# Retention issued ahead of the RWKV projections in a two-layer hybrid backbone

## The chip, the cores and the metric

The kernel runs on one core of one Trainium2 chip. The metric is the device time of one execution in microseconds (us). It is given as the median of several runs; single executions that were profiled carry a trace from which the rows below are taken. TensorE is called PE in the rows, VectorE DVE, ScalarE ACT, GpSimd POOL, and SP is the engine that issues nearly all transfers.

## What is computed

A backbone of two layers (DEPTH 2) over 1024 latent tokens and 256 context tokens of width 1024. Every layer projects the modulated tokens once, feeds four mixers of 256 columns each (mLSTM, Hyena, retention, RWKV-7), joins them by an output projection, and ends with a convolutional feed-forward part. Retention and RWKV-7 are independent of each other; each scans forward and backward. The parts of the reference that matter here:

```python
def token_mixer(u, uc, p, ang, need_ctx):
    parts = split_columns(u @ p['w_in'])
    parts_c = split_columns(uc @ p['w_in'])
    ...
    yr, yr_c = retention_mixer(parts[8:12], parts_c[8:12], ang, gs(2, ng), gs(2, nb))
    yw, yw_c = rwkv_mixer(parts[12:18], parts_c[12:18], p['rwkv_mu'], ...)
    y = jnp.concatenate([ya, yb, yr, yw], -1).astype(u.dtype) @ p['w_out']

# retention, per chunk of 128 tokens
s = jnp.einsum('bhid,bhjd->bhij', qc, kc) * decay_mask
o = jnp.einsum('bhij,bhjd->bhid', s, vc) + jnp.einsum('bhid,bhde->bhie', qc * q_dec[..., None], s_mem)
s_new = s_mem * chunk_dec[:, None, None] + jnp.einsum('bhjd,bhje->bhde', kc * k_dec[..., None], vc)

# the front of RWKV-7
z = token_shift(jnp.concatenate(seq_parts, -1).astype(F32), mu)
r, k, v, wlo, alo, glo = jnp.split(z, list(RWKV_SPLIT), axis=-1)
g = jax.nn.sigmoid(glo) @ g2
kk = kk * lax.rsqrt(jnp.sum(kk * kk, -1, keepdims=True) + 1e-12)
bonus = jnp.sum(rh * kh * rk[None, :, None, :], -1, keepdims=True) * vh
```

The second layer (called layer 1) puts out the latent tokens alone, 8 tiles of 128; layer 0 all 10 tiles.

## The kernel before

`layer` (line 1353) runs the mixers' front one after the other: Hyena, the projections of mLSTM and of retention (which write to memory), then `rwkv_front`, then `retention`, then the scans of RWKV-7 and mLSTM together, the output projection and the feed-forward part. All instructions go through a scheduler that keeps each engine's queue in an order of its own, worked out from a simulated timeline; an engine then executes its queue strictly in that order. The order of the code sets the priority and the order in which buffers are handed out.

`rwkv_front` (line 376) makes seven projections of 128 columns, in the order j = 6, 2, 3, 4, 5, 0, 1. Each is `proj` (line 1050): a weight block is loaded, split into a high and a low part (lines 1015 and 1016), and multiplied in three passes (lines 1022, 1023, 1024) for token blocks of 512, 512 and 256, which makes 72 matmuls; ScalarE moves each block out (line 1061). `seg_conv` (line 347, operations at 352, 354, 355 on VectorE) shifts along the tokens. What follows a projection is deferred behind the next one: for j=6 the gates (matmuls at line 397), for j=2 and 3 the keys and their norms by a matmul with a block of ones (line 406), for j=4 and 5 the values and their transposes (line 1104), for j=0 and 1 the bonus: r is stored to memory (`wrk`, line 415), the key and value are loaded (417, 419), multiplied (418), summed by the ones (matmul 422) and stored (423 to 424 on VectorE).

`retention` (line 796) loads queries, keys and values by 30 transfers (28 in layer 1; line 803). It rotates queries and keys of eight tiles: two products on GpSimd (line 812), two operations on VectorE (813, 814) for each. It forms k2 (818) and multiplies it with the values (matmul 820, copied out at 822) for all ten tiles. GpSimd then scans the states, 16 times a product and a sum (826, 827). Then each tile's output follows: transposes (832, 838), scores (846) masked on VectorE (849), and two products of the scores and the state (852, 853), and after every two tiles a group norm and a store of `yr` (line 659).

After that `close_u` gives back the projected input, `psum` deals out the PSUM banks anew, and `rwkv` begins: it loads what the front stored (`rkk`, line 480, from `wrk`; TWA, VSA), multiplies on VectorE (lines 500 to 530, the product with the loaded keys at 515), transposes a matrix (550), and inverts it step by step (557, 558). The wide scans with which `mlstm` begins (lines 693 to 704) stand on the same VectorE queue.

```python
            rwkv_front(k,l,pv,pvr,last)
            with k.tc.tile_pool(name="rt",bufs=1,side="right") as k.p_rt:
                retention(k,l,last)
        close_u(k)
        psum(k,cbank=2,ybank=1,pbank=1,dbank=2,mbank=2)
```

Of the kernel before, what the change touches and what calls it, by code (L numbers as in the profile page):

```python
# [310 lines left out]
def hyena_proj(K,l,pv,last):  # L311
    NT=8 if last else 10
    for j in range(6):
        z=proj(K,l,1040+j*128,not last,K.bank if l and j<0 else None)
        zc=K.p_tmp.tile([128,1280],F32,tag="tmpA",name="zc",bufs=2)
        w=(pv['hw'][:,j:j+1],pv['hw'][:,6+j:7+j],pv['hw'][:,12+j:13+j],pv['hb'][:,j:j+1])
        seg_conv(K,lambda o,n: zc[:,o:o+n],z,w,ctx=not last)
        later(K,lambda zc=zc,j=j: z_tokens(K,zc,NT,dram=K.D['hyx'][:,j*128:j*128+128],pad=False))
    later(K)
# [38 lines left out]
def rwkv_params(k,l,pv,p):  # L358
    nc=k.nc; tt=nc.vector.tensor_tensor
    c0=p.tile([128,7],F32,name="c0")  # L360
    tt(out=c0,in0=pv['mu0'],in1=pv['mu1'],op=ALU.add)
    nc.vector.tensor_scalar(out=c0,in0=c0,scalar1=-1.0,scalar2=1.0,op0=ALU.mult,op1=ALU.add)
    G2=p.tile([128,256],F32,name="G2"); nc.sync.dma_start(G2[64:128],k.a['rwkv_g2'][l])
    return c0,G2
# [530 lines left out]
def params_mix(k,l,pool):  # L895
    a=k.a
    v1=lambda n: a[n][l:l+1].rearrange("o (j p) -> (o j) p",p=128)
    mu=a['rwkv_mu'][l]
    specs=[('mw',rows(a['mlstm_conv_w'][l]),12),('mb',v1('mlstm_conv_b'),4),('hw',rows(a['hyena_conv_w'][l]),18),('hb',v1('hyena_conv_b'),6),
           ('mu0',rows(mu[0:1]),7),('mu1',rows(mu[1:2]),7),('kk',v1('rwkv_kk'),2),('ka',v1('rwkv_ka'),2),  # L900
           ('rk',a['rwkv_rk'][l:l+1].rearrange("o h d -> (o h d)").rearrange("(j p) -> j p",p=128),2),
           ('ng',v1('out_norm_g'),8),('nb',v1('out_norm_b'),8)]
    return load_rows(k,specs,"pvm%d"%l,pool)
# [394 lines left out]
def open_u(k):  # L1298
    k.ucm=k.tc.tile_pool(name="u",bufs=1,side="right"); pu=k.ucm.__enter__()
    k.uh=pu.tile([128,8,1280],F32R,name="uh"); k.ul=pu.tile([128,8,1280],F32R,name="ul")  # L1300


def close_u(k):
    k.ucm.__exit__(None,None,None)
# [14 lines left out]
def mlstm_proj(k,l,pv,last,js=range(8)):  # L1319
    nc=k.nc; D=k.D; nfull=1024 if last else 1280  # L1320
    for j in js:
        z=proj(k,l,j*128,(not last) or 2<=j<6)
        if j<4:
            t=k.p_tmp.tile([128,1280],F32,tag="tmpA",name="mt",bufs=2)
            seg_conv(k,lambda o,n: t[:,o:o+n],z,(pv['mw'][:,j:j+1],pv['mw'][:,4+j:5+j],pv['mw'][:,8+j:9+j],pv['mb'][:,j:j+1]),ctx=(not last) or j>=2)
            n=1024 if (last and j<2) else 1280
            nc.scalar.activation(out=t[:,:n],in_=t[:,:n],func=ACTF.Silu)
            if j<2: nc.vector.tensor_scalar(out=t[:,:n],in0=t[:,:n],scalar1=0.125,scalar2=None,op0=ALU.mult)
            store_fm(k,D['mqk'][j*128:j*128+128],t,False,n)
        elif j<6: later(k,lambda z=z,j=j: z_tokens(k,z,10,dram=D['mv'][:,(j-4)*128:(j-4)*128+128]))  # L1330
        else:
            later(k)
            n=1025 if last else 1282
            nc.scalar.activation(out=z[:,1:n],in_=z[:,1:n],func=ACTF.Sigmoid)
            store_fm(k,D['go'][(j-6)*128:(j-6)*128+128],z,True,nfull)
    later(k)


def filters(k,l):
    with k.tc.tile_pool(name="hf",bufs=1,side="right") as k.p_hf, k.tc.tile_pool(name="hfy",bufs=1,side="right") as k.p_hy:  # L1340
        for L in ((1024,256) if l==0 else (1024,)): hyena_filter(k,l,L,k.Ds[l]['ks' if L==1024 else 'ksc'])
# [11 lines left out]
def layer(k,l,out):  # L1353
    nc=k.nc; last=l==1
    D=k.D=k.Ds[l]; k.Dn=k.Ds[l+1] if not last else None
    with ExitStack() as es:
        P=lambda **kw: es.enter_context(k.tc.tile_pool(**kw))
        pl=P(name="pl",bufs=1)
        pv=params_mix(k,l,pl)
        with ExitStack() as ed:  # L1360
            P2=lambda **kw: ed.enter_context(k.tc.tile_pool(**kw))
            if l: pg=P2(name="pg",bufs=1)
            k.p_w=P2(name="w",bufs=1); k.p_z=P2(name="z",bufs=1); k.p_tmp=P2(name="tmp",bufs=1)
            if not l: pg=P2(name="pg",bufs=1)
            pvr=rwkv_params(k,l,pv,pg)
            k.bones=pg.tile([128,128],F32,name="bones"); nc.sync.dma_start(k.bones,k.a['c_bones'])
            k.sum16=pg.tile([32,16],F32,name="sum16"); nc.sync.dma_start(k.sum16,k.a['c_sum16'])
            GT=gates(k,l,pg,pl)
            hyena_proj(k,l,pv,last)
            if l>0: filters(k,l)  # L1370
            with k.tc.tile_pool(name="hy",bufs=1,side="right") as k.p_hy:
                hyena(k,l,pv,last)
            mlstm_proj(k,l,pv,last,range(0,8))
            ret_proj(k,l,pv,last,range(0,8))
            rwkv_front(k,l,pv,pvr,last)
            with k.tc.tile_pool(name="rt",bufs=1,side="right") as k.p_rt:
                retention(k,l,last)
        close_u(k)
        psum(k,cbank=2,ybank=1,pbank=1,dbank=2,mbank=2)
        with ExitStack() as ew:  # L1380
            with ExitStack() as er:
                R=lambda **kw: er.enter_context(k.tc.tile_pool(bufs=1,side="right",**kw))
                p1=R(name="r1"); p2=R(name="r2"); pa=R(name="pa"); e3=ExitStack(); p3=e3.enter_context(k.tc.tile_pool(name="r3",bufs=1,side="right"))
                with k.tc.tile_pool(name="ml",bufs=1) as k.p_ml:
                    k.J=k.p_ml.tile([128,128],F32,name="J"); nc.sync.dma_start(k.J,k.a['c_J'])
                    scan=rwkv(k,l,pv,last,p1,p2,p3)
                    for _ in range(2): next(scan)
                    side=ada_steps(k,[(l,g) for g in range(2,6)]+[(1,g) for g in range(2) if l==0],pa,k.mbank,17 if last else 19)
                    mlstm(k,l,GT,last,side)
                pw=ew.enter_context(k.tc.tile_pool(name="pw",bufs=1))  # L1390
                wo=[[pw.tile([128,1024],F32R,name="wo%d%d"%(q,i)) for i in range(2)] for q in range(8)]
                for _ in scan: pass
                e3.close()
                load_wo(k,l,wo,p2.tile([128,8,256],F32,tag="G",name="wst",bufs=3))
                ep=ExitStack(); pb=ep.enter_context(k.tc.tile_pool(name="pb",bufs=1))
            psum(k,bank=5,dbank=3)
            open_u(k)
            mix_out(k,l,pv,last,wo,pl,pb,ep)
    ffn(k,l,last,out)
# [46 lines left out]
```

## Time and profile before

| | |
|---|---|
| time, median of 3 runs | 4264.0 us (4252.06 to 4266.33) |
| the profiled execution: own time | 4269.9 us |
| its span, first to last instruction | 4268.0 us |
| granted TensorE clock, mean | 0.940 |
| PE busy | 3956.8 us (93%) |
| DVE busy | 2672.2 us (63%) |
| ACT busy | 1416.9 us (33%) |
| POOL busy | 979.7 us (23%) |

The shares are means over the whole span, over stages of very different kinds. The granted clock is the share of TensorE's full speed that the chip allowed; its levels are 1.2 and 2.4 GHz. A row of the timeline that stands for several instructions gives the time from the first's start to the last's end, and the starts of two rows tell how long the first really held the engine, since matmuls overlap. A single-precision matmul of the code stands as two in the trace, so the 40 key-value products of line 820 are 80 there.

### The profile page before, as it was taken

What the parts mean: (1) busy time and instruction counts of PE and PEld (TensorE: products, weight loads), DVE (VectorE), ACT (ScalarE), POOL (GpSimd) and SP (SyncE); (2) the same over time, 40 slices, a digit from 0 to 9 for tenths busy, and PEclk for the clock granted to TensorE, in tenths of its full rate; (3) what the DMA queues carried; (4) which work ended last, traced back from release to release, by engine and by line L of the source; (5) the groups of instructions that cost most, each with busy time, mean ns of one, the idle gap of its engine ahead of it and who ended that gap; (6) DMA issues with size and microseconds to landing.
All of it is one profiled execution on the core that took longest, in us unless ns stands there. A gap on an engine that the chain in (4) does not pass through costs nothing.

```text
span 4268.0 us, 65334 instructions
## 1 busy us (share of the span) xinstructions
PE 3956.8 (93%) x24976; PEld 3210.9 (75%) x24976; DVE 2672.2 (63%) x5412; ACT 1416.9 (33%) x2855; POOL 979.7 (23%) x2158
## 2 busy tenths in 40 slices
PE   5999999699979999999997999996899899999998
PEld 3878877566668888888884688885666678888886
DVE  5655665789769444444449555676888684444447
ACT  4433343554344211211123433344544342112121
POOL 3320023466512000000021221024666320000002
PEclk6999999789989999999998999997899699999999
DMA  4235444343343111111113235553332431111112
GB/s 166 74 102 177 149 153 122 112 143 116 122 160 119 45 40 34 41 40 35 37 35 124 82 91 154 169 162 114 122 115 84 136 114 55 48 41 55 45 50 99
DMA packets 477138, 414.16 MB, mean 97 GB/s; under 512 B 48827, under 2 KB 443284, under 8 KB 474010
## 3 DMA queue, kind: packets, MB, share of 16 engines
q1 hardware_dynamic: 476826, 409.99, 31.0%
q8 instruction: 197, 3.23, 0.3%
q14 instruction: 115, 0.94, 0.1%
HBM read 323.65 MB, written 86.25 MB: 96 GB/s over the span
## 4 chain that ended last, share of the span: by engine, by line
PE 52%; DVE 11%; DMA 3%; issue 2%; POOL 1%; ACT 1%; SPq 0%; ACTq 0%; DVEq 0%; POOLq 0%
PE bank L1022 9%; PE bank L1023 9%; PE bank L1024 9%; PE dbank L1022 6%; PE dbank L1023 6%; PE dbank L1024 6%; DVE bst L983 1%; DMA xt<-x 1%; DVE facc L1205 1%; PE bank L186 1%; PE bank L187 1%; DMA wst<-in_w_out 1%; PE dbank L529 0%; DVE facc L1206 0%; DVE facc L1274 0%
## 5 line engine op out<-in xcount | busy, mean ns | idle before, releaser
L1022 PE MATMUL dbank<-uh,wh 128*128 128x512 f32 (+1 forms) x2120 | 765.3, 370 | 8.8 <-ACT tmpB L398 5.7
L1023 PE MATMUL dbank<-ul,wh 128*128 128x512 f32 (+1 forms) x2120 | 761.2, 368 | 0.0
L1016 DVE TENSOR_TENSOR wl<-wst,wh 128x1024 fp32r<-128x1024 f32 x146 | 185.5, 1272 | 491.9 <-ACT wh L1015 367.3
L1024 PE MATMUL dbank<-uh,wl 128*128 128x512 f32 (+1 forms) x2120 | 480.6, 367 | 0.0
L1022 PEld LDWEIGHTS dbank<-uh,wh 128*128 128x128 f32 x2120 | 401.4, 189 | 85.0 <-ACT tmpB L398 6.1
L1023 PEld LDWEIGHTS dbank<-ul,wh 128*128 128x128 f32 x2120 | 401.6, 189 | 68.9 <-issue 1.1
L1024 PEld LDWEIGHTS dbank<-uh,wl 128*128 128x128 f32 x2120 | 365.9, 188 | 70.5 <-issue 1.5
L1264 DVE TENSOR_TENSOR facc<-facc,bank 128x512 f32<-128x512 f32 x324 | 221.8, 686 | 205.1 <-PE bank L1024 205.1
L1022 PE MATMUL bank<-uh,wh 128*128 128x512 f32 (+1 forms) x920 | 334.9, 372 | 4.5 <-ACT uh L1010 4.5
L1233 POOL MEMSET fz<- 128x1 f32 x132 | 7.2, 98 | 1433.6 <-DVE fc L1248 1433.6
L1023 PE MATMUL bank<-ul,wh 128*128 128x512 f32 (+1 forms) x920 | 335.1, 372 | 0.8 <-DVE ul L1011 0.8
L1022 PE MATMUL bank<-wdh,gh 128*128 128x512 f32 x792 | 314.9, 400 | 17.9 <-DVE facc L1278 8.7
L1023 PE MATMUL bank<-wdl,gh 128*128 128x512 f32 x792 | 310.5, 392 | 1.0 <-DVE wdl L1016 1.0
L1024 PE MATMUL bank<-wdh,gl 128*128 128x512 f32 x792 | 248.1, 392 | 0.0
L1015 ACT ACTIVATE wh<-wst 128x1024 fp32r<-128x1024 f32 x146 | 154.8, 1060 | 238.1 <-PE dbank L1023 168.4
L1015 ACT ACTIVATE wdh<-wst 128x1024 fp32r<-128x1024 f32 x46 | 48.8, 1062 | 529.4 <-PE bank L1024 427.7
L558 POOL TENSOR_TENSOR XL<-XL,lt 128x48 f32<-128x48 f32 (+26 forms) x620 | 204.4, 330 | 47.7
L557 POOL TENSOR_TENSOR lt<-LM,XL 128x48 f32<-128x48 f32 (+26 forms) x620 | 187.1, 302 | 119.4 <-ACT XL L551 45.0
L1024 PE MATMUL bank<-uh,wl 128*128 128x512 f32 (+1 forms) x920 | 211.9, 372 | 0.0
L1022 PEld LDWEIGHTS bank<-uh,wh 128*128 128x128 f32 x920 | 174.1, 190 | 36.1 <-ACT uh L1010 5.6
L1023 PEld LDWEIGHTS bank<-ul,wh 128*128 128x128 f32 x920 | 174.2, 189 | 31.9 <-DVE ul L1011 1.7
L1022 PEld LDWEIGHTS bank<-wdh,gh 128*128 128x128 f32 x792 | 149.7, 189 | 59.4 <-DVE facc L1278 14.9
(476 smaller groups left out, 8132.3 us busy)
## 6 DMA issues: line engine op xcount, KB each, us to landing
wst<-in_ffn_w_up SPq DMA_DIRECT2D x88, 512.0 KB
adaw<-in_ada_w SPq DMA_DIRECT2D x160, 256.0 KB
wst<-in_w_in SPq DMA_DIRECT2D x58, 512.0 KB
wst<-in_ffn_w_down SPq DMA_DIRECT2D x46, 512.0 KB
df<-in_c_F SPq DMA_DIRECT2D x10, 1344.0 KB
xt<-x SPq DMA_DIRECT2D x26, 512.0 KB
df<-in_c_I SPq DMA_DIRECT2D x8, 1344.0 KB
rkk<-wrk SPq DMA_DIRECT2D x10, 1024.0 KB
```

The costliest lines, as they stand in the source:

```text
L186: mm(dst_re,F[:,i],pre(slot),start=True,stop=False); mm(dst_re,F[:,i+1],pim(slot),start=False,stop=True)
L187: mm(dst_im,F[:,i],qim(slot),start=True,stop=False); mm(dst_im,F[:,i+2],qre(slot),start=False,stop=True)
L557: e.tensor_tensor(out=t_,in0=LM[:,j,j+1:32].unsqueeze(2).to_broadcast([128,n,m]),in1=X[h][:,j:j+1,0:m].to_broadcast([128,n,m]),op=A.mult)
L558: e.tensor_tensor(out=X[h][:,j+1:32,0:m],in0=X[h][:,j+1:32,0:m],in1=t_,op=A.add)
L983: for h in range(2): nc.vector.bn_stats(out=st[:,h],in_=x[h])
L1015: k.nc.scalar.activation(out=h,in_=st,func=ACTF.Copy)
L1016: k.nc.vector.tensor_tensor(out=lo,in0=st,in1=h,op=ALU.subtract)
L1022: mm(ps,lh,rh,start=(i==0),stop=False)
L1023: mm(ps,lh,rl,start=False,stop=False)
L1024: for i,((lh,ll),(rh,rl)) in enumerate(pairs): mm(ps,ll,rh,start=False,stop=(i==n-1 and more is None))
L1205: for o,i,gg in zip([y[:,h] for h in hs],x,[g[:,h] for h in hs]) if parts else [(y,x,g)]: stt(out=o,in0=i,scalar=m,in1=gg,op0=ALU.subtract ...
L1264: else: tt(out=d,in0=d,in1=ps,op=ALU.add)
```

## The change

`rwkv_front` is called after `retention` instead of before it, inside the scope of retention's buffers. It is the same in both layers. The buffers of retention therefore live until the front is through. Nothing else is edited.

```diff
             ret_proj(k,l,pv,last,range(0,8))
-            rwkv_front(k,l,pv,pvr,last)
             with k.tc.tile_pool(name="rt",bufs=1,side="right") as k.p_rt:
                 retention(k,l,last)
+                rwkv_front(k,l,pv,pvr,last)
         close_u(k)
         psum(k,cbank=2,ybank=1,pbank=1,dbank=2,mbank=2)
```

What the scheduler makes of it on PE, in layer 0 behind the projection j=2: line 397 is the gates, line 820 the key-value products (`k_...` is the k2 of one tile), lines 1022 and 1023 the projection j=3. The piece is the difference, and goes on with 71 more matmuls of j=3 taken out here.

```order
 L397 MATMUL dbank<-tmpA,G_1691 128x512 x2
 L397 MATMUL dbank<-tmpA,G_1691 128x256
+L820 MATMUL bank<-rqkv_5194,k_5228 128x64 x4
+L820 MATMUL bank<-rqkv_5194,k_5237 128x64 x4
+L820 MATMUL bank<-rqkv_5194,k_5256 128x64 x4
+L820 MATMUL bank<-rqkv_5194,k_5274 128x64 x4
 L397 MATMUL dbank<-tmpA,G_1691 128x512 x2
 L397 MATMUL dbank<-tmpA,G_1691 128x256
-L1022 MATMUL dbank<-uh,wh 128x512
-L1023 MATMUL dbank<-ul,wh 128x512
```

Behind them in the new order stand the other six groups of line 820, with one pair of the projection's matmuls in between, then the first transposes of retention's tiles (832, 838), and from there on one tile of retention for about every 24 matmuls of the projections j=3, 4 and 5. The projections j=0 and 1 and the bonus of both come last. In layer 1 seven of the ten groups stand behind the projection j=4 and before the norm matmuls of j=3.

SP's queue in layer 0, at the end of the front: `wrk` is the memory that holds r, k and kk (line 415 stores r of j=0 and then j=1, line 480 loads them as `rkk`). Before:

```order
L415 DMA wrk_100<-tmpA 1280x1x128
L1125 DMA bv_93<-tmpB 128x1280
L417 DMA tmpB<-wrk_100 64x10x128 x2
L419 DMA tmpB<-wvf_102 128x1280
L1125 DMA bv_93<-tmpB 128x1280
L659 DMA yr_88<-rqkv_6024 128x2x256 x4
L479 DMA TWA<-twa_103 64x128 x2
L659 DMA yr_88<-rqkv_6024 128x2x256
L1385 DMA J<-in_c_J 128x128
L480 DMA rkk<-wrk_100 128x2048
```

Now:

```order
L415 DMA wrk_100<-tmpA 1280x1x128
L1125 DMA bv_93<-tmpB 128x1280
L484 DMA VSA<-wv_101 64x2x256
L484 DMA SV<-wv_101 64x2x256
L479 DMA TWA<-twa_103 64x128 x2
L480 DMA rkk<-wrk_100 128x2048
```

The stores of `yr` have moved ahead, among the stores of the front, and the load of `rkk` stands a few transfers behind the store of r (j=1), where five stores of `yr` and the bonus of j=1 stood between before.

VectorE's queue in layer 0, around the transposition of line 550, before (lines 697 to 704 belong to mLSTM):

```order
L697 TENSOR_TENSOR mVO<-mIG,mB 8x1280
L696 TENSOR_TENSOR mVO<-mB,mM 8x1280
L530 TENSOR_TENSOR G<-dbank,rmask 128x512
L702 TENSOR_TENSOR me<-mB,mM 8x10
L503 TENSOR_TENSOR lw<-cs 128x520
L515 TENSOR_TENSOR bk<-bk,rkk 128x4x64 x2
L700 TENSOR_TENSOR mW<-mVO,mM 8x1280
L515 TENSOR_TENSOR bk<-bk,rkk 128x4x64 x2
L703 TENSOR_TENSOR me<-me,mM 8x10
L704 TENSOR_TENSOR mIG<-mVO,me 8x1280
L550 STREAM_TRANSPOSE LM<-NB 128x1024
```

and now (lines 423 and 424 are the bonus of j=1):

```order
L423 TENSOR_TENSOR tmpB<-dbank,tmpB 128x512 x2
L423 TENSOR_TENSOR tmpB<-dbank,tmpB 128x256
L500 SCALAR_TENSOR_TENSOR lw<-ex,lw 128x8x64
L424 TENSOR_SCALAR tmpB<-tmpB,pvm_1661 128x1280
L502 SCALAR_TENSOR_TENSOR cs<-smask,lw 128x260 x2
L530 TENSOR_TENSOR G<-dbank,rmask 128x512 x2
L503 TENSOR_TENSOR lw<-cs 128x520
L535 STREAM_TRANSPOSE NB<-G 32x128 x4
L671 CAST identb<-ident 128x128
L530 TENSOR_TENSOR G<-dbank,rmask 128x512 x2
L550 STREAM_TRANSPOSE LM<-NB 128x1024
L557 TENSOR_TENSOR lt<-LM,XL 128x15
```

The mLSTM operations (lines 693 to 704) have moved behind line 550, and the bonus of j=1 stands before it.

## Rows read from the trace of the kernel before

**Rows 1.** The page, part 4, of the whole span: the chain's shares by engine.

```profile
PE 52%; DVE 11%; DMA 3%; issue 2%; POOL 1%; ACT 1%; SPq 0%; ACTq 0%; DVEq 0%; POOLq 0%
```

**Rows 2.** Windows: start:end, length, busy us (count) by engine, PE clock, DMA, GB/s.

```profile
580.47:608.70 28.23, 28.23 (x146) 23.69 (x144) 13.17 (x15) 15.69 (x18) 1.29 (x9) 1.00 0.64 197
608.70:640.00 31.30, 25.62 (x115) 19.43 (x115) 30.45 (x47) 11.76 (x22) 22.63 (x37) 0.89 0.50 151
640.00:707.00 67.00, 67.00 (x371) 56.73 (x370) 37.12 (x44) 24.27 (x41) 22.16 (x30) 1.00 0.51 134
707.00:764.00 57.00, 50.56 (x338) 42.64 (x336) 32.79 (x62) 19.69 (x41) 22.01 (x29) 0.85 0.25 81
764.00:806.00 42.00, 18.78 (x146) 15.37 (x147) 32.75 (x51) 26.76 (x58) 15.95 (x28) 0.72 0.62 167
800.00:1000.00 200.00, 172.65 (x2084) 131.05 (x2085) 175.13 (x551) 102.46 (x313) 129.91 (x373) 0.86 0.42 129
2838.00:2858.00 20.00, 19.67 (x110) 16.38 (x110) 17.90 (x27) 11.02 (x18) 12.30 (x21) 1.00 0.95 286
2888.50:2944.00 55.50, 46.74 (x311) 38.64 (x309) 35.67 (x59) 19.75 (x42) 29.28 (x37) 0.85 0.26 79
```

**Rows 3.** Timeline of PE: start, length, instruction, xcount, [idle before, its releaser].

```profile
608.70 4.56 PE L397 MATMUL dbank<-tmpA,G 64*128 64x512 f32 x12
618.94 0.79 PE L1022 MATMUL dbank<-uh,wh 128*128 128x512 f32 x1 [5.67 <-ACT tmpB L398]
...
654.51 1.89 PE L820 MATMUL bank<-rqkv,k 128*128 128x64 f32 x16
...
723.14 0.69 PE L853 MATMUL bank<-rSS,rT 128*128 128x64 f32 x2 [2.10 <-POOL rSS L827]
...
738.56 0.60 PE L832 MATMUL bank<-ident,rqkv 128*128 128x128 f32 x4
...
742.79 0.61 PE L832 MATMUL bank<-ident,rqkv 128*128 128x128 f32 x4
...
2837.82 2.31 PE L406 MATMUL dbank<-tmpB,bones 128*128 128x512 f32 x6
```

**Rows 4.** Timeline of DVE from 608 to 636: first rotation, a convolution, last rotation.

```profile
609.27 0.66 DVE L813 TENSOR_TENSOR rqkv<-rqkv,crcos 128x256 f32<-128x256 f32 x1 [1.89 <-DMA rqkv<-rqkv]
609.86 1.47 DVE L354 SCALAR_TENSOR_TENSOR tmpA<-z,pvm,tmpA 128x1024 f32<-128x1024 f32 x1
...
635.18 0.43 DVE L814 TENSOR_TENSOR rqkv<-rqkv,rtmp 128x256 f32<-128x256 f32 x1
```

**Rows 5.** Groups by line, DVE, from 608.7 to 636: the k2 products.

```profile
L818 DVE TENSOR_TENSOR k<-rqkv,crKD 128x512 f32<-128x512 f32 x4 | 3.4, 874 | 0.0
```

**Rows 6.** Groups by line, POOL: 608.7 to 764, then (layer 1) 2841 to 2918.

```profile
L812 POOL TENSOR_TENSOR rtmp<-rqkv,crsin 128x128 f32<-128x128 f32 x32 | 21.1, 688 | 14.5 <-DMA rqkv<-rqkv 11.1 <-issue 2.5 <-POOL rtmp L812 0.8
L827 POOL TENSOR_TENSOR rSS<-rSS,rst 64x256 f32<-64x256 f32 x16 | 18.4, 1151 | 29.3 <-ACT rSS L822 28.3
L826 POOL TENSOR_TENSOR rst<-rSS,crCD 64x256 f32<-64x256 f32 x16 | 14.6, 912 | 4.7 <-issue 3.6
...
L827 POOL TENSOR_TENSOR rSS<-rSS,rst 64x256 f32<-64x256 f32 x16 | 14.9, 930 | 1.2
```

**Rows 7.** Timeline of SP's queue: a store to wrk, the load from it.

```profile
711.78 0.56 SPq L415 DMA_DIRECT2D wrk<-tmpA  x1
...
771.72 0.42 SPq L480 DMA_DIRECT2D rkk<-wrk  x1
```

**Rows 8.** Timeline of DVE behind layer 0's retention.

```profile
778.24 1.42 DVE L515 TENSOR_TENSOR bk<-bk,rkk 128x256 f32<-128x256 f32 x4
...
786.17 2.80 DVE L693 TENSOR_TENSOR_SCAN mB<-cmask,mLF 8x1280 f32<-8x1280 f32 x1
...
803.08 1.47 DVE L704 TENSOR_TENSOR mIG<-mVO,me 8x1280 f32<-8x1280 f32 x1
804.48 1.94 DVE L550 STREAM_TRANSPOSE LM<-NB 128x1024 f32<-128x1024 f32 x1
```

## The prediction

> **What bounds the kernel now.** I read the page's chain of waits first [rows 1]: 52% of it is TensorE, 11% VectorE, 1% GpSimd. The change touches the end of the mixers' front, about 155 us in layer 0 and 135 us in layer 1, so the next view is the stretches there, cut at the places where the work changes [rows 2]. Two projections take 28.23 us (14.1 each) with TensorE full. From 608.70 on, layer 0's stretches hold TensorE 25.62 of 31.30 us busy, 67.00 of 67.00 and 50.56 of 57.00: 12.1 us idle, at granted clocks 0.89, 1.00 and 0.85. With the two levels 1.2 and 2.4 GHz, 0.85 means about 17 of the 57 us at the lower one, of which 6.4 are the idle time; the other 10.7 are matmuls that cost 5.3 us more than at 2.4 GHz. The first stretch gives 0.6 in the same way. So before the change about 18.0 of the 155.3 us between 608.70 and 764.00 are lost, and about 137.3 us of TensorE work remain. In layer 1 the last stretch is alike, 46.74 of 55.50 busy at 0.85.
>
> Then the instructions of TensorE one by one [rows 3]: the first loss is 5.67 us at 618.94, behind the gate matmuls; the others are waits of the first retention tiles, the last of them 2.10 us at 723.14 for the state that GpSimd scans (line 827). From 738.56 to 742.79 one steady tile of retention takes 4.23 us. What the front's last matmuls release is read from VectorE after 764 [rows 8]: the product with the loaded keys at 778.24, then the transposition of the scan's matrix (line 550) at 804.48, with which the serial inverse of the RWKV part can begin. From 764.00 to 806.00 TensorE is busy for only 18.78 us [rows 2], so that stretch is a chain of transfers and VectorE and not of matmuls.
>
> **The change, part by part.** No instruction's arithmetic changes; I count the moved ones.
>
> *Keys and values first.* In the order of before, the 72 matmuls of projection j=3 stand right behind the gates on TensorE, and the key-value products are spread behind later projections. In the new order all ten groups of them (line 820) stand there, with one pair of the projection's matmuls between. Each needs its k2 from VectorE, which needs the rotation. VectorE ran that rotation all but without a gap, from 609.27 to 635.61 [rows 4] (30.45 of 31.30 us busy in that stretch, [rows 2]), 26.3 us with four of the k2 products (874 ns each, [rows 5]) and the segment convolution of j=2 in it. The other six k2 add 6 x 0.874 = 5.2 us. So the last product becomes possible at about 640. TensorE has until then the gates, 4.56 us by [rows 3], the ten groups of key-value products (16 of the passes take 1.89 us from 654.51, 0.11 each without the last one's tail, so 80 take 8.7), and one pair: some 14 of 31 us. It idles about 16 us, and 1.5 more go at the lower clock (between the 0.6 and the 5.3 above). Lower end 8 us, if the 5.7 that was idle there anyway is the core of it; upper end 19. The cover that is lost is the projection j=3, 14.1 us, which now comes later, where it can in turn cover the retention tiles.
>
> *The scan.* GpSimd does 32 rotation products, 688 ns each, and then 16 + 16 scan operations [rows 6]: 18.4 + 14.6 = 33.0 us in layer 0. With the 930 ns that line 827 takes in layer 1 it is 14.9 + 14.6 = 29.5. Before, the scan ran beside five projections and was waited for by 2.1 us. Now its last products are done at about 636 and it ends at 665 to 669, while TensorE, with about 17 us of projection and transposes after 640, stands before the first product with the state (line 853) at about 657. The wait is 8 to 12 us, I take 9, and 1.5 for the clock. Nothing excludes less, since the tiles need the states one by one and the first tile's may be early: lower end 2.
>
> The difference in rates between the layers' scans (1151 and 930 ns for line 827, [rows 6]) is not a difference of work. The Trainium skill, "SBUF — State Buffer", "SBUF: two separate sides", states that GpSimd and a VectorE instruction with two SBUF operands exclude each other on a shared port pair, the later one waiting for the other's whole instruction. By that rule a fuller VectorE beside the scan lengthens it above 33 us and the wait above 12; by the rows it lies between 29.5 and 33.0, and the sum goes by those.
>
> *The tiles.* All ten tiles (42.3 us of TensorE) now lie between projections, about one per 24 matmuls, so the 6.4 us of idle time and the 5.3 at the lower clock behind 707 go. That is the gain.
>
> *The sum at the last projection.* 155.3 - 18.0 = 137.3 us of work; the two bone products of j=0 and j=1 now stand behind the last projection matmul (2.2 us each, from the 2.31 us that six of j=3 take at 2837.82, [rows 3], the last one's tail left out), so 132.9 remain. With 16 + 1.5 + 9 + 1.5 = 28 us lost the last projection ends at 608.7 + 132.9 + 28 = 769.6, against 764.0 for the end of retention before.
>
> *The transfer behind it.* Before, the last keys and queries went to memory at 711.78 and were loaded again at 771.72 [rows 7], 60 us apart, so that trip was hidden. SP reached the load when the last output store of retention had drained. Now the stores of retention come early, and the load waits for z, the segment convolution, the store and the load itself. From 764.0 to the product at 778.24 [rows 8] were 14.2 us, of which 6.5 lie behind the load's issue at 771.72. The new chain has these 6.5, a store of the same kind and size before them, at most 6.5 too, and an eviction and the last block's convolution, about 3 us (one long operation, line 354, takes 1.47, [rows 4], and the last block is a quarter as wide in three operations). That is 13 to 16; I take 15.5. Ends 10 and 20, the lower if the two transfers are half as long as the bound. The product then comes at about 785, 7 us late.
>
> *VectorE behind it.* On its queue j=1's rest (lines 418, 423, 424, some 4.4 us) now stands before line 550, and six wide mLSTM operations, 2.80 us the first and 1.47 the last [rows 8], 11.5 us in all, stand after it instead of before. These nearly balance: line 550 ends at about 812 instead of 806.4, +5.5. The 11.5 us are owed later, beside the inverse. From 800 to 1000 VectorE is busy for 175.13 of 200 us [rows 2], so 0 to 11.5 of it counts; I take 3, since 25 us of slack in that stretch are twice the work. Layer 0 thus loses 5.5 + 3 = **8.5 us**.
>
> *Layer 1.* There the key-value products move before j=3's bones: from 2838 TensorE was 19.67 of 20.00 us busy [rows 2] while the rotation ran, and now only some 6 us of products are possible in it. Idle 14, and 2 to 4 for the clock; the scan, by the same reckoning as above, costs 4 to 7 us. Against these stand the 8.8 us idle in the last stretch and, with 0.30 x 55.5 = 16.7 us at the lower clock, half of the other 7.9, thus 12.7 us that go, and the two bone products (4.4) that move behind. What was 2944.0 becomes 2947 to 2953, and with the same chain behind it line 550 is 4 to 10 us late, by these 3 to 9 and the balance of VectorE's queue. With 2 to 3 of the owed VectorE work I take **+9.5**.
>
> Together +18 us. The profiled execution's own time is 4269.9, so 4287.9, a ratio of 1.0042; it stands 5.9 us above the median of 4264.0, to which the ratio gives **4282**.
>
> **The rivals.** *Retention fills what it costs (no change).* The scheduler's queues put the key-value products early, but the rotation is faster without convolutions between, the scan's early states suffice, and the idle time is 8 instead of 16 and the wait 2 instead of 9. Then the loss is 13 us instead of 28, the last projection ends at 755, the chain costs 20 instead of 14, and each layer comes out at -4 to +5: 4256 to 4274. For it: the states are needed one by one. Against: VectorE had no gap from 609 to 636.
>
> *Dense work keeps the clock (faster).* If the projections cover the retention waits throughout, losses fall to the order of 6 us in each layer, the last projection ends at 608.7 + 132.9 + 6 = 748, and the product with the keys at 763: 13 to 15 us earlier per layer, -26, which is 4238. It decides itself at the ten key-value groups: it needs their k2 ready by about 620, where VectorE had two tiles of eight rotated. The Trainium skill, "TensorE: Matmul & The Clock Gate", "HAM oscillation", says that idle gaps between small groups of matmuls pay the lower clock again each time; mixing tiles with projections is what it favours. The granted clock of 0.85 behind 707 [rows 2] agrees, and bounds this part at 5.3 us a layer.
>
> *The owed VectorE work ends last (much slower).* If the mLSTM scans delay the mLSTM part and that part ends the mixer, the whole 11.5 us counts in each layer, +18 + 2 x 8.5 = +35: 4299, and with the upper ends of both waits 4310.
>
> That the scheduler undoes the new order is excluded by the order itself, which has moved on every engine.
>
> **How the numbers follow.** A measurement of this kernel tells 0.3%, 12.8 us, from no change. Chances: forecast 0.40 (its own range 4277 to 4294), no change 0.33 (4251 to 4277), faster 0.15, much slower 0.12. Forecast and much slower make slower 0.52; same is 0.33 and faster 0.15. The range that should hold 8 in 10 takes in the no-change case, the upper part of the faster one and the lower part of the last: 4248 to 4304.
>
> **What would show it.** Right: a hole of 12 to 19 us on TensorE before the key-value products at 613 to 640 and in layer 1 from 2838 on, released by VectorE's line 818; a wait of 5 to 12 us for line 827; no waits of that kind later, and a granted clock near 1.00 through the tiles; the load of the keys at once behind the store of j=1, and line 550 at 807 to 815 and, in layer 1, 2989 to 2997 (less what layer 0 shifts). Wrong: TensorE full from 620 on; or line 550 before 800; or a layer 0 that ends earlier although line 550 is late, which would mean that the chain behind it has slack.

## The result, and the profile after

The changed kernel takes **4323.95 us** (median of 4 runs, 4319.48 to 4324.59); the kernel before, run beside it, 4258.03 (4249.41 to 4266.33). The ratio is **1.015**, with a 95% interval of 1.0136 to 1.0164: 66 us slower, where +18 was forecast, and outside the range.

The profiled execution took 4324.59 us. The page's head and the shares of its chain of waits answer to [rows 1]; the shares are almost the same and tell nothing of the cause.

```profile
span 4322.8 us, 65356 instructions
...
PE 50%; DVE 12%; issue 3%; DMA 2%; POOL 2%; ACT 2%; SPq 0%; DVEq 0%; ACTq 0%; POOLq 0%
```

The spans differ by 4322.8 - 4268.0 = 54.8 us and not by 66, since the profiled execution of the kernel before (4269.9 us) was 11.9 us above the median that stands here. Layer 1 begins 33.1 us late (the last store of yh, just ahead of its front, is issued at 2852.71 instead of 2819.64), so 33.1 of them come from layer 0 and 21.7 from layer 1.

**The front ended when it was forecast to.** Windows of the changed kernel, layer 0, columns as in [rows 2], cut where its work changes:

```profile
608.70:640.00 31.30, 25.26 (x97) 20.59 (x95) 30.92 (x48) 11.37 (x25) 24.09 (x36) 0.60 0.53 164
640.00:669.00 29.00, 21.60 (x114) 18.79 (x115) 7.46 (x10) 5.23 (x10) 20.32 (x28) 0.79 0.00 1
669.00:707.00 38.00, 38.00 (x248) 32.40 (x247) 21.62 (x39) 22.25 (x35) 3.23 (x6) 0.94 0.29 80
707.00:768.00 61.00, 60.89 (x356) 51.47 (x355) 26.17 (x38) 21.82 (x36) 4.46 (x10) 1.00 0.43 117
768.00:806.00 38.00, 19.85 (x82) 14.16 (x81) 29.86 (x60) 16.16 (x38) 13.67 (x24) 0.73 0.72 211
```

The first two rows hold the two losses, the third and fourth the gain: retention's tiles between projections run with TensorE full, at a granted clock of 0.94 and 1.00, where [rows 2] has 0.85 behind 707. The waits are in the timeline of TensorE (columns as in [rows 3]):

```profile
615.37 7.06 PE L820 MATMUL bank<-rqkv,k 128*128 128x64 f32 x32 [3.92 <-DMA rqkv<-rqkv]
...
638.69 1.94 PE L820 MATMUL bank<-rqkv,k 128*128 128x64 f32 x8 [2.12 <-issue]
...
662.41 0.69 PE L853 MATMUL bank<-rSS,rT 128*128 128x64 f32 x2 [7.40 <-POOL rSS L827]
```

The 80 passes of the key-value products run at the lower clock here: the first 32 take 7.06 us, all of them some 18. The scan, in groups of GpSimd's instructions from 608.7 to 680, against [rows 6]:

```profile
L827 POOL TENSOR_TENSOR rSS<-rSS,rst 64x256 f32<-64x256 f32 x16 | 13.4, 836 | 1.2
L826 POOL TENSOR_TENSOR rst<-rSS,crCD 64x256 f32<-64x256 f32 x16 | 11.0, 687 | 1.5 <-ACT rSS L822 0.4
```

**What came behind it was not as forecast.** VectorE's timeline in the changed kernel, against [rows 8]:

```profile
785.23 2.41 DVE L515 TENSOR_TENSOR bk<-bk,rkk 128x256 f32<-128x256 f32 x4 [2.86 <-DMA rkk<-wrk]
...
801.77 0.88 DVE L424 TENSOR_SCALAR tmpB<-tmpB,pvm 128x1280 f32<-128x1280 f32 x1
...
809.66 2.00 DVE L550 STREAM_TRANSPOSE LM<-NB 128x1024 f32<-128x1024 f32 x1 [1.38 <-ACT NB L536]
...
817.92 2.85 DVE L693 TENSOR_TENSOR_SCAN mB<-cmask,mLF 8x1280 f32<-8x1280 f32 x1
...
836.67 1.47 DVE L704 TENSOR_TENSOR mIG<-mVO,me 8x1280 f32<-8x1280 f32 x1
```

The RWKV part's line 550 ends 5.2 us late, as reckoned. But mLSTM's first scan (line 693) begins 31.7 us late, and line 704 is 33.6 us late: all of mLSTM, not its VectorE operations alone, starts that much later. The queue of SP shows why. First the changed kernel: the end of the front (the two halves of r to wrk by line 415, the bonus of each half to bv), then mLSTM's first load, of J.

```profile
761.68 0.55 SPq L415 DMA_DIRECT2D wrk<-tmpA  x1
...
774.19 0.55 SPq L415 DMA_DIRECT2D wrk<-tmpA  x1
775.21 0.35 SPq L1125 DMA_DIRECT2D bv<-tmpB  x1
...
779.74 0.51 SPq L480 DMA_DIRECT2D rkk<-wrk  x1
...
781.66 1.26 SPq L417 DMA_DIRECT2D tmpB<-wrk  x2
...
794.59 0.54 SPq L419 DMA_DIRECT2D tmpB<-wvf  x1
...
802.68 0.33 SPq L1125 DMA_DIRECT2D bv<-tmpB  x1
805.67 0.34 SPq L1385 DMA_DIRECT2D J<-in_c_J  x1
```

The last eviction of a projection is at 768.16, the last bonus store 34.5 us later: the load of that half's keys (line 417), the product (418), another load (419), ones-matmul (422), 423, 424. GpSimd's first instruction of mLSTM names what it had waited for:

```profile
805.82 0.18 POOL L667 MEMSET mV<- 128x40 f32 x1 [7.87 <-DMA bv<-tmpB]
```

mLSTM's buffers lie where the front's buffers lie, and are free only when the last store has read tmpB. In the kernel before, the bonus was stored at 732.60, beside retention; the place was given back by retention's last store (SP's load of J waited for it, by the list of its waits), and J was loaded 34.4 us earlier than now (SP's queue, kernel before):

```profile
732.60 0.33 SPq L1125 DMA_DIRECT2D bv<-tmpB  x1
...
769.13 0.36 SPq L659 DMA_DIRECT2D yr<-rqkv  x1
771.32 0.35 SPq L1385 DMA_DIRECT2D J<-in_c_J  x1
```

From line 704 to the last store of ym it takes 416.5 us in both kernels (803.08 to 1219.59, 836.67 to 1253.18; it is no fixed length, e5 below has 405.7), and that store ends the mixer of layer 0: the chain of waits of the kernel before goes through it to the load of the output projection's weights.

```profile
1219.59 2.12 DMA ym<-gq
1222.73 0.55 DVE wo L1016 x2
1223.28 2.15 DMA wst<-in_w_out
```

Layer 1 is alike at its start: line 704 32.3 us and line 550 6.9 us late, counted from the last store of yh. Its end is another. There RWKV's last store of yw ends the mixer, 54.5 us behind mLSTM's last store of ym in the kernel before and 39.6 in the changed one; it is 21.2 us late by the same count, the store of ym 36.1. The chain of waits goes through it to the output projection's first input, first in the kernel before, then in the changed one:

```profile
3387.30 2.12 DMA yw<-gq
3389.53 1.06 ACT uh L1157
```
```profile
3441.60 2.14 DMA yw<-gq
3443.84 1.07 ACT uh L1157
```

RWKV's own chain gets later on the way: the first line 550 by 6.9 us, the second by 17.0. The six wide operations of mLSTM, which stood ahead of both, now stand between them, among the steps of the inverse, and the two lie 44.2 us apart where it was 34.1 (timeline of VectorE, the kernel before, then the changed kernel):

```profile
2984.93 1.93 DVE L550 STREAM_TRANSPOSE LM<-NB 128x1024 f32<-128x1024 f32 x1
...
3019.07 1.97 DVE L550 STREAM_TRANSPOSE LM<-NB 128x1024 f32<-128x1024 f32 x1 [0.66 <-POOL lt L557]
```
```profile
3024.92 1.93 DVE L550 STREAM_TRANSPOSE LM<-NB 128x1024 f32<-128x1024 f32 x1
...
3031.22 2.81 DVE L693 TENSOR_TENSOR_SCAN mB<-cmask,mLF 8x1280 f32<-8x1280 f32 x1
...
3048.89 1.47 DVE L704 TENSOR_TENSOR mIG<-mVO,me 8x1280 f32<-8x1280 f32 x1
...
3069.13 1.91 DVE L550 STREAM_TRANSPOSE LM<-NB 128x1024 f32<-128x1024 f32 x1 [2.76 <-POOL lt L557]
```

The front's windows in layer 1, where its losses lie:

```profile
2870.00:2900.00 30.00, 23.18 (x101) 19.83 (x100) 29.75 (x47) 13.38 (x23) 21.72 (x34) 0.66 0.55 159
2900.00:2930.00 30.00, 21.86 (x142) 19.40 (x141) 17.84 (x19) 8.16 (x16) 26.16 (x32) 0.82 0.39 98
```

### The profile page after: what moved, and what is told of

The parts are those of the page before. It is cut to its first block, busy times and chain, and to the rows that moved or that the text cites. A ratio compares the mean times of both kernels' runs of the same rounds, so it can differ in the third digit from the quotient of the medians.

```text
span 4322.8 us, 65356 instructions
## 1 busy us (share of the span) xinstructions
PE 3976.6 (92%) x24976; PEld 3227.8 (75%) x24976; DVE 2670.3 (62%) x5412; ACT 1425.4 (33%) x2861; POOL 994.6 (23%) x2158
## 4 chain that ended last, share of the span: by engine, by line
PE 50%; DVE 12%; issue 3%; DMA 2%; POOL 2%; ACT 2%; SPq 0%; DVEq 0%; ACTq 0%; POOLq 0%
PE bank L1023 8%; PE bank L1022 8%; PE bank L1024 8%; PE dbank L1022 6%; PE dbank L1023 6%; PE dbank L1024 6%; DVE bst L983 1%; DMA xt<-x 1%; DVE facc L1205 1%; PE bank L186 1%; DVE mt L1167 1%; PE bank L187 1%; PE dbank L529 1%; PE mbank L973 0%; DVE xt L1205 0%
## 5 line engine op out<-in xcount | busy, mean ns | idle before, releaser
L557 POOL TENSOR_TENSOR lt<-LM,XL 128x48 f32<-128x48 f32 (+26 forms) x620 | 198.1, 320 | 137.1 <-ACT XL L551 49.0
L558 POOL TENSOR_TENSOR XL<-XL,lt 128x48 f32<-128x48 f32 (+26 forms) x620 | 214.1, 345 | 47.5
```

Of the source, the lines that this page charges most:

```text
L557: e.tensor_tensor(out=t_,in0=LM[:,j,j+1:32].unsqueeze(2).to_broadcast([128,n,m]),in1=X[h][:,j:j+1,0:m].to_broadcast([128,n,m]),op=A.mult)
L558: e.tensor_tensor(out=X[h][:,j+1:32,0:m],in0=X[h][:,j+1:32,0:m],in1=t_,op=A.add)
```

## The experiments

The theory: the loss is mLSTM's late start, behind the bonus that is now the last thing of the front. The rivals: the holes in TensorE's work, or the late load of `rkk` behind the last projection. Every ratio is against the kernel before on the same chip. The table holds what was measured; a delay is an instruction's start against the kernel before, less the shift of the last store of yh ahead of the front, in layer 0: line 704 (mLSTM), line 550 (RWKV), and the first uh of line 1010, which is the first tile that comes out of the output projection behind the mixer. (The projection's own first input, line 1157, is 33.1 us late in the changed kernel.)

| kernel | median us, ratio [95%] | 704 | 550 | uh |
|---|---|---|---|---|
| the changed kernel | 4323.95, 1.0150 [1.0136, 1.0164] | 33.3 | 4.8 | 36.2 |
| e1 layer 0 only | 4307.62, 1.0111 [1.0095, 1.0126] | 34.5 | 6.2 | 40.7 |
| e2 layer 1 only | 4277.08, 1.0044 [1.0032, 1.0057] | 0.7 | 0.7 | -3.6 |
| e3 after, no bonus | 4277.02, 1.0045 [1.0031, 1.0059] | 8.1 | 10.1 | 9.5 |
| e4 before, no bonus | 4292.82, 1.0077 [1.0063, 1.0091] | 18.8 | 23.8 | 20.6 |
| e5 before, mLSTM held | 4282.58, 1.0047 [1.0031, 1.0063] | 19.2 | -8.1 | 9.6 |
| e6 after, j=6 last | 4303.93, 1.0093 [1.0077, 1.0110] | 22.4 | 24.3 | 23.2 |
| e7 before, j=6 last | 4319.62, 1.0136 [1.0108, 1.0164] | 12.1 | 17.1 | 17.8 |
| e8 retention before j=5, j=6 last | 4295.57, 1.0070 [1.0052, 1.0088] | 5.8 | 7.7 | 21.2 |
| e9 retention before j=0 | 4278.38, 1.0024 [1.0008, 1.0040] | -2.9 | -0.9 | 16.2 |
| e10 after, own buffers | 4305.15, 1.0113 [1.0094, 1.0131] | 27.7 | 11.3 | 23.7 |
| e11 before, own buffers | 4300.58, 1.0101 [1.0086, 1.0116] | -3.8 | 24.2 | 18.7 |
| e13 scan before j=4 | 4298.27, 1.0084 [1.0062, 1.0106] | 5.1 | 7.0 | 16.5 |
| e14 e13, own buffers | 4294.65, 1.0090 [1.0076, 1.0105] | -24.7 | 3.5 | 6.8 |
| e15 e9, own buffers | 4287.44, 1.0050 [1.0035, 1.0065] | -14.9 | 14.0 | 15.6 |
| e16 bonus early | 4278.43, 1.0034 [1.0017, 1.0051] | 0.9 | 2.9 | 4.4 |

Each delay is from one execution, and it moves where nothing was edited too: e1's layer 1, in which the calls stand in the old order, has line 704 11.7 and line 550 16.7 us late, and its uh 0.5 us early.

**One layer at a time.** e1 takes the new order in layer 0 alone, e2 in layer 1.

```diff
-            rwkv_front(k,l,pv,pvr,last)
+            if l!=0: rwkv_front(k,l,pv,pvr,last)
...
-                retention(k,l,last)
+                retention(k,l,last); l==0 and rwkv_front(k,l,pv,pvr,last)
```

> The new order in layer 0 alone. Theory A (the mLSTM part starts late because its buffers are those of the front, which the last bonus store gives back 34 us later, and the end of mLSTM holds the weights of layer 0's output projection): about +34 us against the kernel before (4290 to 4296), with the first wide mLSTM scan (line 693) near 818 and the last store of ym near 1253. Theory B (only TensorE's holes in the front count, and mLSTM has slack): +5 to +9 us.

> The new order in layer 1 alone. Theory A: mLSTM starts about 27 us late there too, but RWKV and not mLSTM ends that mixer, so less than in layer 0: about +20 us. Theory B: the same as in layer 0, +5 to +9 us. If both parts add up to the measured 60 us or so, the layers do not help or harm each other.

They lose 49.6 and 19.1 us, together 68.7 against the 66: the losses add, and the larger lies in layer 0, more than the 34 that were expected there. In e1 alone mLSTM's delay reaches the end of the mixer whole.

**The tail.** e3 is the changed kernel without the bonus: lines 416 to 424 left out, r itself stored in its place. e4 does the same to the kernel before, as a control.

```diff
-                kk=T5("tmpB")
...
-                store_fm(k,D['bv'][ft*128:ft*128+128],bv,False,NL)
+                store_fm(k,D['bv'][ft*128:ft*128+128],t,False,NL)
```

> The changed kernel without the bonus's tail: for j=0 and 1 the load of k, the product, the ones matmul, the product with v and the bias are left out, and r itself is stored in place of the bonus. The front's buffers are then given back some 10 us behind the last projection (768), not 38. Theory A: line 693 stands near 790 instead of 818, and the time is 4265 to 4285, so 40 to 60 us of the difference go. Theory B: the holes in the front remain, 4305 to 4320.

> The control: the kernel before without the same bonus tail. Its mLSTM start waits for retention's last store and not for the bonus, so both theories: 0 to -8 us against the kernel before (4.4 us of matmuls and some 9 us of VectorE fewer per layer, most of them hidden).

e3 takes back 47 of the 66 us, with the holes and the late load of `rkk` still there (line 550 is 10.1 us late, more than in the changed kernel). J follows the last store, and line 693 comes at 798.09 instead of 817.92 (SP's queue and VectorE's timeline of e3):

```profile
775.29 0.80 SPq L1125 DMA_DIRECT2D bv<-tmpA  x1
782.09 0.54 SPq L1385 DMA_DIRECT2D J<-in_c_J  x1
```
```profile
798.09 2.80 DVE L693 TENSOR_TENSOR_SCAN mB<-cmask,mLF 8x1280 f32<-8x1280 f32 x1
```

The control was a miss: with less work it was 35 us slower. Its windows show retention's tiles, now without the bonus's ones-matmuls among them, at the lower clock of 1.2 GHz while TensorE is all but full; the kernel before ran the same stretch at 2.4 GHz. First e4, then the kernel before:

```profile
707.00:740.00 33.00, 23.84 (x135) 21.27 (x134) 13.06 (x27) 9.66 (x19) 18.40 (x27) 0.68 0.20 64
740.00:764.00 24.00, 24.00 (x101) 21.31 (x100) 6.85 (x15) 5.26 (x12) 1.04 (x1) 0.50 0.03 12
764.00:790.00 26.00, 23.90 (x103) 21.28 (x101) 7.85 (x18) 6.00 (x14) 2.09 (x2) 0.50 0.07 23
```
```profile
740.00:764.00 24.00, 23.78 (x187) 21.23 (x185) 12.15 (x29) 10.27 (x24) 3.59 (x4) 1.00 0.10 34
```

So e4 doesn't price the bonus's own work, and e3's 47 us hold that work too: they don't price the wait alone.

**The late start alone.** e5 is the kernel before, in which mLSTM's first gates take a bias of zero that is made from the first LM, so that mLSTM waits for line 550. In layer 0 the order of TensorE and of VectorE up to 765 us stays that of the kernel before; the wide scans move behind line 550.

```diff
+    zt=p.tile([8,1],F32,name="mzt"); nc.gpsimd.tensor_scalar(out=zt,in0=K.lmx[0:8,0,0:1],scalar1=0.0,scalar2=None,op0=A.mult)
...
-        act(out=IG[:,i0*128:(i0+n)*128],in_=b[0:8,:n*128],func=ACTF.Copy)
+        act(out=IG[:,i0*128:(i0+n)*128],in_=b[0:8,:n*128],func=ACTF.Identity,bias=zt)
```

> The kernel before, with nothing changed but that the first gates of mLSTM also wait for the first transposed matrix of RWKV (line 550), by a bias of zero times one of its elements. It delays mLSTM alone: with the wide scans behind it, line 550 comes some 8 to 11 us earlier, and line 693 at about 800 to 808 instead of 786. Theory A (mLSTM's start sets layer 0's end one for one): layer 0 ends 14 to 22 us later, layer 1 up to 10 us, together +15 to +30 us. Theory B (mLSTM has slack, RWKV's start counts): -5 to -10 us, since line 550 is earlier.

Held by 19.2 and 19.5 us in the two layers, the kernel loses 16.2 us by the medians and 20 by the ratio, though line 550 is 8.1 and 8.7 us earlier, having VectorE to itself. A late start alone costs, then, but at 0.42 to 0.52 us for one; by that rate the 33.3 + 32.3 us of the changed kernel are 28 to 34 of its 66. It is not one for one, as theory A had it: in the profiled execution layer 0 ends 9.2 us later, where 14 to 22 were expected, and layer 1 takes 0.5 us less than before.

**The buffers.** In e10 the six wide rows of mLSTM that come first have a pool of their own, which does not lie over the front's last buffers; e11 does it to the kernel before.

```diff
-                with k.tc.tile_pool(name="ml",bufs=1) as k.p_ml:
+                with k.tc.tile_pool(name="ml0",bufs=1) as q0, k.tc.tile_pool(name="ml",bufs=1) as q1:
...
```

> The changed kernel with mLSTM's buffers in two pools: the six wide rows that its scans use lie in a pool of their own, 30 KB, over the buffers of the projection's weights and z, and no longer wait for the bonus's store; the rest waits as before. Nothing is left out, TensorE's order in the front is the same. Theory A: the end of mLSTM's scans (line 704) comes 10 to 16 us earlier than in the changed kernel (near 822 instead of 837), and layer 0's end by as much; together with layer 1 -15 to -30 us against the changed kernel, 4295 to 4310. Theory B: no change against the changed kernel, 4320 to 4328.

> The kernel before with the same two pools. There the front is through at 733, so the scans can run beside retention, where VectorE has room. Theory A: line 704 near 785 instead of 803 and line 550 up to 10 us earlier, layer 0 10 to 18 us shorter, together -15 to -30 us against the kernel before. Theory B (slack): -3 to +3.

By its ratio e10 loses 48 us and so takes back 18. J is loaded at 775.30 instead of 805.67, but the gate product that reads it stands in TensorE's queue behind the first products of RWKV (line 529), and these behind the bonus's (timeline of TensorE in e10):

```profile
802.18 3.64 PE L529 MATMUL dbank<-AR,bk 128*128 128x256 f32 x8 [2.03 <-issue]
805.75 0.40 PE L686 MATMUL mbank<-ident,GT 128*8 128x128 f32 x4
805.97 0.39 PE L687 MATMUL mbank<-J,GT 128*8 128x128 f32 x4
```

In the changed kernel line 687 first runs at 808.94, 3.0 us later. So the buffers are the first wait and the in-order queue a second one right behind it; both hang on the tail. But e10 does not show what the wait for the buffers costs: its first wide scan (line 693), counted as in the table, is 31.4 us late, as late as in the changed kernel, and line 704 only 5.6 us earlier, where 10 to 16 were expected. Most of the 18 us must come from somewhere else, which was not found. e11 was a miss of e4's kind: line 693 came at 755.4, in the middle of retention's tiles; these waited 5.75 us for VectorE (line 849, at 762.86), ran on at the lower clock and ended 27 us late (windows of e11):

```profile
740.00:760.00 20.00, 17.12 (x170) 13.75 (x168) 11.94 (x18) 10.46 (x21) 2.21 (x2) 1.00 0.05 15
760.00:780.00 20.00, 17.14 (x72) 15.38 (x73) 10.03 (x16) 8.91 (x12) 3.16 (x2) 0.52 0.08 27
780.00:800.00 20.00, 16.75 (x74) 15.02 (x72) 6.30 (x14) 3.98 (x9) 2.08 (x2) 0.50 0.05 16
```

**Other orders.** e6 and e7 put j=6, which has no bonus, last in the new and the old order. e8, e9 and e16 issue retention in the middle of the seven projections; e13 does so with its scan alone, and its tiles after them; e14 and e15 add the own buffers to e13 and e9.

```diff
-    for j in (6,2,3,4,5,0,1):
+    for j in (2,3,4,5,0,1,6):
```
```diff
-        z=proj(k,l,2832+j*128,True); ft=j%2
+        j==5 and mid(); z=proj(k,l,2832+j*128,True); ft=j%2
...
-                retention(k,l,last)
+                rwkv_front(k,l,pv,pvr,last,lambda: retention(k,l,last))
```

(The first with the changed kernel's calls is e6, with the old calls e7, with the second diff e8. e9 has `j==0` there and the order unchanged; e16 `j==5` and the order 2, 4, 0, 3, 5, 1, 6; e13 `j==4` and a `yield` in retention behind the scan.)

> The changed kernel with the projections in the order 2, 3, 4, 5, 0, 1, 6, so that the gates and not the bonus come last; nothing is left out. The front's buffers come free about 12 us behind the last projection instead of 38. Theory A: line 693 near 793, ym's last store 8 to 14 us late instead of 33, and the time 4272 to 4288. Theory B: 4310 to 4320, as the holes at the key-value products and the state remain.

> The control: the kernel before with the same order 2, 3, 4, 5, 0, 1, 6. Theory A: mLSTM's start waits for retention's last store as before, so -5 to +5 us, unless the tail of retention loses TensorE's clock as in the run without the bonus (granted clock 0.50 to 0.60 from 707 on), then up to +20 a layer.

> Order 2, 3, 4, 5, 0, 1, 6, with retention issued in the middle, ahead of the projection j=5: the first three projections cover rotation and key-value products, the last four the tiles. Theory A: no hole before the key-value products, the last projection ends near 750 to 756, and mLSTM's start at 775 to 785: 4245 to 4265. If instead the time stays over 4290, the mixing itself is what costs.

> Retention is issued between the projections: behind j=5 and ahead of j=0 and 1, in the front's own order. Rotation and key-value products lie under five projections, as in the kernel before, and two projections can fill the tiles' waits. The last projection ends near 751 to 757 and the bonus some 37 us later, so mLSTM's scans are through (line 704) at 812 to 822 (+10 to +19), while line 550 comes at 793 to 803 (0 to -10). If both starts share the end of layer 0 as in the runs so far, about half of the one and a third of the other count: +5 to +15 a layer, 4265 to 4285. If only mLSTM's start counted: +20 to +40; if only TensorE's holes in the front counted: -10 to -20.

> Only the first part of retention is moved ahead (rotation, key-value products, scan of the state), and only ahead of the projection j=4; the tiles stay behind the front as in the kernel before, and so does the bonus. The state is scanned by about 700 instead of 725, so the tiles do not wait for it, and keep the clock: retention ends 5 to 10 us earlier in each layer, and with it mLSTM's and RWKV's starts. Theory A: -8 to -20 us against the kernel before. If the early key-value products hold TensorE before j=4, or the clock is lost in the tail all the same, 0 to +20.

> Both of the last two together: state early, two pools. If the two gains are independent, their sum: -20 to -45 us against the kernel before.

> The same with mLSTM's scans in the pool of their own, so that they do not wait for the bonus. Line 704 at 790 to 805, line 550 as in the run without it or 5 us later. Shared starts: 8 to 20 us less than the run without the second pool, 4250 to 4270. If mLSTM's start has no part in it: no difference between the two.

> Projections in the order 2, 4, 0, 3, 5, 1, 6, retention issued ahead of j=5: the first bonus is through early, the second lies under j=6. Line 704 at 800 to 810 and line 550 at 805 to 815, as the gates are last and stand ahead of RWKV's first matmuls: 4270 to 4295. If only TensorE's holes counted: -10 to -20 against the kernel before.

No order beats the kernel before. Where retention lies among the projections and the bonus's tail no longer holds mLSTM (e9, e16), the loss is down to 10 and 14 us by the ratios (15 by the medians), and line 704 of layer 0 is within 3 us of its old place. e6 brought mLSTM only 11 us forward, since its last block stores gw from the same buffer (793 to 798). e14 is the sharpest against a simple story: mLSTM starts 24.7 us earlier than before, and the mixer still ends 6.8 us later. And e15, with mLSTM 12 us ahead of e9's, is the slower of the two.

Nine of the fifteen kernels (e1, e4, e6, e7, e8, e11, e13, e14, e15) came out slower than was expected of them. By its own sentence e8, at 4295.57, says that the mixing itself costs. The account below is one of the changed kernel; it does not forecast the time of another order.

In every layer that has line 693 behind its first line 550 (the changed kernel, e1's layer 0, e2's layer 1, e5 and e10), the first two transpositions of line 550 lie 44.1 to 49.4 us apart, against 34.6 and 34.1 in the two layers of the kernel before and 30.2 to 42.3 in the other layers. So the wide operations cost RWKV's chain some 10 to 15 us where they stand in it.

## Why the prediction was wrong

- *The holes of the front: right in sum, wrong in what they are made of.* Of the first window 6.0 us are idle, and 0.60 means that 25.0 of its 31.3 us are at the lower clock, so 19 of matmuls that cost 9.5 more: 15.5, forecast 17.5. But 16 of these were to be idle, in a hole of 12 to 19 us that line 818 releases, and 1.5 the clock. No such hole came: the waits are 3.92 us for a load and 2.12 with no releaser named, and the 80 key-value passes took 18 us where I had counted 8.7. That the split was wrong did no harm, since VectorE set the end of the stretch: its last k2 was done at 638.6 and the last group of products ran at 638.69, for which I had reckoned 640. The second has 7.4 idle and 2.4 by the clock, 9.8, forecast 10.5. The other two hold 2.4. Together 27.7 us, against 28.
- *The last projection, the transfer, line 550: right.* 768.2 (forecast 769.6), the product with the keys at 785.2 (785), line 550's end at 811.7 (812). In layer 1 line 550 is 6.9 us late (4 to 10), though its terms were off as well: the wait before the key-value products is 4.26 us, where 14 were to be idle, and that for line 827 8.12 (4 to 7).
- *The scan's rate:* 836 ns where [rows 6] has 1151 and 930: it was faster, beside an emptier VectorE (7.46 of 29 us busy); that the one makes the other was not tried. The prediction's bounds held the wait all the same.
- *"VectorE behind it": wrong, and this is the step that failed.* It took the six wide mLSTM operations as 11.5 us of **work**, "owed later, beside the inverse", of which 0 to 11.5 would count, 3 taken, because VectorE had 25 us of slack from 800 to 1000. They are the **beginning of a chain**. By the same paragraph they would follow line 550, so mLSTM would begin some 26 us late; slack in the engine that does the work says nothing of what the chain behind it loses. It began 31.7 us late, since its buffers and its gate products waited for the bonus's last store, 34.5 us behind the last projection. That wait was not priced: I counted lines 418 to 424 as 4.4 us of VectorE and not as three transfers in a row. In layer 0, which mLSTM ends, the delay came through whole (33.3 at line 704, 33.3 at the last store of ym, 36.2 at uh); the layer lost 33.1 us where the sum had 8.5. In layer 1, which RWKV ends, the same step failed in another way: the work was not hidden in the slack but paid in RWKV's chain, 10.1 us between the first two of line 550 where 2 to 3 were taken, and the layer lost 21.7 us for 9.5. That this is the cause in layer 1 is read from the traces and was not tried by itself.
- *The rivals.* "Retention fills what it costs" needed 8 us idle and a wait of 2; the two stretches lost 15.5 and 9.8. "The owed VectorE work ends last" named the right place in layer 0 and the wrong price (at most 11.5 us in each layer, +35); in layer 1 mLSTM does not end the mixer. "Dense work keeps the clock" was right in its mechanism, 1.00 from 707 to 768, and didn't decide: its saving is inside the 27.7 above.

**What stays open.** The delay alone, at e5's rate, is 28 to 34 of the 66 us; the 47 of e3 hold the bonus's work too. In layer 1 e5 held mLSTM by 19.5 us and its uh was 0.7 us early, so the late start by itself does not explain what the changed kernel loses there. A straight line through all 17 profiled kernels gives, in layer 0, a delay of uh of 9.4 + 0.46 x (704) + 0.35 x (550), to 7.6 us (root mean square), and in layer 1 of -1.7 + 0.39 x + 0.39 x, to 5.8. The standard errors of the two factors are 0.13 and 0.22 in layer 0, 0.12 and 0.15 in layer 1, so that of line 550 in layer 0 is not clear of nothing. That both beginnings count because the two chains share engines until the mixer's end is a reading of it and not a test. For the changed kernel that is 26 and 13 us of 36 and 22. What the rest is was not settled, nor what the 9.4 us are: e9 loses 16.2 us in layer 0 with both beginnings in time.

## What to carry to other kernels

Price a moved step by when the chain behind it can **start**, and not only by how much work changes place: find the first instruction of the next phase, and list the buffers and queue places that it must wait for. Where phases share memory, the last store of one is the start of the next, so look at the tail that the phase put last has behind its last matmul: with the gates and not the bonus last (e6) the same order of phases lost 38 us and not 66. Work that is owed is not free because its engine has slack: find the chain of that engine that it will stand in. And a store that was hidden in the middle of the old order (the bonus at 732.60) has to be followed to its new place with every load, product and store on its way.

## What the runs showed of the hardware

The lower clock outlived the stall that began it. In e4, after a wait of 5.87 us, TensorE was busy for 24.00 of 24 and 23.90 of 26 us on retention's thin matmuls and the granted clock stayed at 0.50; in the kernel before, after a wait of 2.10 us, it came back behind six of the bonus's ones-matmuls (line 422, 4.58 us from 726.18): two of the tile's products took 0.63 us up to 725.33 and 0.39 from 731.53. That these matmuls brought it back was not tried by itself, and they don't keep it: in e1's layer 1 the tiles ran at 2.4 GHz behind the bonus's last ones-matmuls (line 422, 3.78 us from 2952.58), waited 1.82 us at 2968.72, and were at the lower clock from 2971 to their end, without a gap (windows of e1):

```profile
2970.00:2985.00 15.00, 15.00 (x66) 13.38 (x64) 3.94 (x9) 3.88 (x9) 1.04 (x1) 0.52 0.11 36
2985.00:2999.00 14.00, 14.00 (x63) 12.58 (x61) 3.86 (x9) 2.44 (x6) 1.04 (x1) 0.50 0.03 11
```

So the lower clock at this place is not owed to the edits of e4 and e11 alone. The Trainium skill, "TensorE: Matmul & The Clock Gate", "What's actually happening", says that activity releases the throttle; here it stayed on while the profile shows TensorE as busy. e4 and e11, whose tiles ran so, came out 35 and 43 us slower than the kernel before; that the clock made the whole of this was not tried.
